# Gathered rows spread to the end of an expert loop, and late fetches begun in its last part and paced by product columns

## The chip, the cores and the metric

One core of one Trainium2 chip runs the whole program. The metric is the device time of one execution in microseconds (us). Engines are named as in the profile: PE (TensorE; PEld its weight loads), DVE (VectorE), ACT (ScalarE), POOL (GpSimd), SP (SyncE, which here issues most DMAs).

## The reference

Two transformer blocks follow one another on 512 tokens, in four tiles of 128, with a width of 1024. What the change touches is the expert layer of the first block and what comes behind it:

```python
def peer_experts(xc, idx, gates, u, v):
    u_sel = jnp.take(u, idx, axis=0)
    act = jax.nn.gelu(jnp.einsum("chkd,cd->chk", u_sel, xc))
    v_sel = jnp.take(v, idx, axis=0)
    return jnp.einsum("chk,chkd->cd", act * gates, v_sel)
...
    x = x + FFN_RESIDUAL_WEIGHT * swiglu(rms_norm_2(x, ffn1_norm[l]), ffn1_w_gate[l], ffn1_w_up[l], ffn1_w_down[l])
    h = rms_norm_2(x, mix_norm[l])
    proj = h @ w_in[l]
    (q_lat, kv_lat, k_rope, fq, fk, fv, f_logit, g_mla, g_fox) = jnp.split(proj, split_points, axis=-1)
```

Each token chooses 128 of the experts (8 heads, 16 each). An expert is a row of u and a row of v, 1024 wide.

## The kernel before

**The expert layer** treats the four tiles in three ways. For three of them the activations of all experts are computed as products with u, 128 experts at a time (`u_tile`, `u_steps`), 128 such groups. Slots 0 and 1 then multiply them by the gates (`hf`, split into `hh` and `hl`) and by v, also group by group: these are the V products in PSUM (`acc`). The gathered tile (GT = 3) uses neither: for each of its 128 choices one indirect DMA on POOL's queue fetches for 128 tokens the row of peer_u (`gather_u`), DVE makes the dot product, and later a second one fetches the row of peer_v (`gather_v`), which DVE adds into `c.ht[GT]`. A fetch is 128 x 1024 floats, 512 KB, into a buffer of tag row, of which there are four. The late tile (LT = 2) takes part in the u products, but its activations are spilled to memory (`act_d`), and class `Late` fetches them back by token, one column of 128 x 1 an indirect DMA (`fetch`, into `c.lact`), and the row of peer_v that belongs to it (`vrow`), which DVE adds into h_late (`add`). `Late.steps(n)` does n of these fetches, acts up to 16 (`AHEAD`) before rows.

**The loop.** u products run 36 (LAG) groups ahead of V products; the loop over i has both until group 91 and V products alone in its last 36 iterations. Behind each iteration `spent(n)` asks for as many of the 256 gathers as n is of `GSPAN`. A weight tile (512 KB) is split into a high half on ACT (wh, L98) and a low half on DVE (wl, L103); `hh` and `hl` have three buffers. Every eighth iteration loads the gates `gt`, 1 MB.

**Behind the loop** `features` transposes the three tiles into feature-major rows, and ffn1 follows for these three: 44 products of 24 matmuls (`mm`, 384 columns) for gate and up, alternately, and eight columns (`dn`) of 66. `Late.steps` is called in both, and then in attention's beginning, until the late tile is complete; from there on it runs by itself as a fourth tile (`last`, L1129 by the wt tiles, full fp32).

**In attention** the products of the late tile are `todo[0]` (the latent part lat of 360 columns, tile tl in the profile: query and key latents, k_rope, forget logits) and `todo[1]` to `todo[3]` (fq, fk, fv), each made by `last` in one of two PSUM banks of tag mm. Then come four z gates, and after them in the code the norms of lat, its transposes (L1218 to L1225), rope, the log-sigmoid of the forget logits (lf, L1240 to L1254) and its running sum cp (L1257).

**Order.** Instructions are put in order at build time by a scheduler that simulates a timeline, engine by engine; `keep_in_program_order` pins the indirect DMAs among each other, which share POOL's queue. Semaphores do the rest at run time, and each engine works in order.

## Time and profile before

| what | value |
| --- | --- |
| median of 3 runs | 2740.44 us (2737.12 to 2742.59) |
| profiled execution | 2743.67 us, its span 2741.5 us |
| mean granted PE clock | 0.964 |
| PE, DVE, ACT, POOL busy | 2546.8, 1815.2, 914.9, 822.2 us |

The span runs from the first instruction to the last one of the profiled execution. Busy time is summed over an engine's instructions; an engine can be busy 93% of the span and still set the end in some stages only, so the stages are read one by one. By the trace the u and V loop with both kinds of products runs until 1335, V products alone until 1433, ffn1 until 1786, and attention's last products of the late tile until about 2145.

### The profile page before, as it was taken

What the parts mean: (1) busy time and instruction counts of PE and PEld (TensorE: products, weight loads), DVE (VectorE), ACT (ScalarE), POOL (GpSimd) and SP (SyncE); (2) the same over time, 40 slices, a digit from 0 to 9 for tenths busy, and PEclk for the clock granted to TensorE, in tenths of its full rate; (3) what the DMA queues carried; (4) which work ended last, traced back from release to release, by engine and by line L of the source; (5) the groups of instructions that cost most, each with busy time, mean ns of one, the idle gap of its engine ahead of it and who ended that gap; (6) DMA issues with size and microseconds to landing.
All of it is one profiled execution on the core that took longest, in us unless ns stands there. A gap on an engine that the chain in (4) does not pass through costs nothing.

```text
span 2741.5 us, 34004 instructions
## 1 busy us (share of the span) xinstructions
PE 2546.8 (93%) x12098; PEld 2088.0 (76%) x12098; DVE 1815.2 (66%) x3710; ACT 914.9 (33%) x1531; POOL 822.2 (30%) x686
## 2 busy tenths in 40 slices
PE   8979988998999989999998988888998999999999
PEld 7955455787888888889878888887444877788887
DVE  7986996997878877874676777776113675443322
ACT  4232011453333333344453322233013554422321
POOL 0000244333444444420006888672000340211100
PEclk9989999999999999999999999998999899999999
DMA  4213138889999989985664778786885313222232
GB/s 173 93 62 102 62 104 280 297 288 324 348 326 339 345 317 331 342 301 176 202 205 132 270 267 269 263 275 230 297 286 176 102 36 108 93 93 100 90 104 75
DMA packets 196921, 567.77 MB, mean 207 GB/s; under 512 B 23240, under 2 KB 60488, under 8 KB 194576
## 3 DMA queue, kind: packets, MB, share of 16 engines
q1 hardware_dynamic: 132464, 355.60, 38.1%
q0 software_dynamic: 59392, 201.42, 21.2%
q10 hardware_dynamic: 4896, 8.57, 0.8%
q8 instruction: 96, 1.57, 0.2%
q14 instruction: 73, 0.60, 0.1%
HBM read 534.05 MB, written 31.47 MB: 206 GB/s over the span
## 4 chain that ended last, share of the span: by engine, by line
PE 63%; DMA 13%; DVE 11%; POOL 6%; issue 5%; ACT 2%; SPq 0%; POOLq 0%; DVEq 0%; ACTq 0%
PE u L419 13%; DMA wf<-u_t 5%; DMA vrow<-peer_v,lidx 5%; PE v L79 4%; PE v L80 4%; PE v L81 3%; PE mm L79 3%; PE mm L80 3%; PE mm L81 3%; POOL lact L715 3%; PE x L960 3%; DMA row<-peer_u,gidx 2%; POOL vrow L735 2%; PE pj L79 2%; PE pj L81 2%
## 5 line engine op out<-in xcount | busy, mean ns | idle before, releaser
L103 DVE TENSOR_TENSOR wl<-wf,wh 128x1024 fp32r<-128x1024 f32 (+2 forms) x438 | 532.5, 1216 | 251.7 <-ACT wh L98 244.9
L98 ACT CAST wh<-wf 128x1024 fp32r<-128x1024 f32 (+2 forms) x438 | 452.9, 1037 | 593.3 <-PE mm L80 163.2
L419 PE MATMUL u<-xh,wh 128*128 128x384 f32 x760 | 267.1, 351 | 38.7 <-ACT wh L98 38.7
L81 PE MATMUL mm<-hh,wl 128*128 128x384 f32 (+1 forms) x704 | 262.0, 372 | 22.6 <-DVE wl L103 22.6
L419 PE MATMUL u<-xh,wl 128*128 128x384 f32 x760 | 265.5, 349 | 8.5 <-DVE wl L103 8.5
L79 PE MATMUL mm<-hh,wh 128*128 128x384 f32 (+1 forms) x704 | 261.0, 372 | 4.3 <-DVE rows L683 2.3
L419 PE MATMUL u<-xl,wh 128*128 128x384 f32 x760 | 264.1, 347 | 0.0
L80 PE MATMUL mm<-hl,wh 128*128 128x384 f32 (+1 forms) x704 | 262.6, 373 | 0.0
L564 POOL DMA_INDIRECT row<-peer_u,gidx x128 | 171.3, 1338 | 251.5 <-DVE jkd L567 226.7
L575 POOL DMA_INDIRECT row<-peer_v,gidx x128 | 173.5, 1355 | 206.8 <-DVE h_tok L578 188.3
L80 PE MATMUL v<-wl,hh 128*128 128x512 f32 x512 | 204.1, 399 | 0.0
L81 PE MATMUL v<-wh,hl 128*128 128x512 f32 x512 | 200.7, 393 | 0.0
L724 DVE SCALAR_TENSOR_TENSOR h_late<-vrow,lact,h_late 128x1024 f32<-128x1024 f32 x128 | 164.4, 1284 | 54.2 <-DMA vrow<-peer_v,lidx 53.4
L419 PEld LDWEIGHTS u<-xh,wh 128*128 128x128 f32 x760 | 149.4, 197 | 46.7 <-ACT wh L98 42.8
L567 DVE SCALAR_TENSOR_TENSOR jkd<-row,xg 128x1024 bf16<-128x1024 f32 x128 | 156.5, 1222 | 37.9 <-DMA row<-peer_u,gidx 37.3
L419 PE MATMUL u<-xf,w 128*128 128x384 f32 x496 | 172.8, 499 | 6.8 <-ACT spill L427 6.8
L735 POOL DMA_INDIRECT vrow<-peer_v,lidx x128 | 155.9, 1218 | 46.4 <-issue 29.3
L81 PEld LDWEIGHTS mm<-hh,wl 128*128 128x128 f32 x704 | 135.9, 193 | 40.1 <-DVE wl L103 25.1
L578 DVE SCALAR_TENSOR_TENSOR h_tok<-row,gwt,h_tok 128x1024 f32<-128x1024 f32 x128 | 163.9, 1280 | 3.5 <-DMA row<-peer_v,gidx 2.7
L715 POOL DMA_INDIRECT lact<-act_d,laid x128 | 153.9, 1203 | 38.8 <-issue 35.3
L419 PEld LDWEIGHTS u<-xh,wl 128*128 128x128 f32 x760 | 148.9, 196 | 14.7 <-DVE wl L103 14.5
L525 POOL TENSOR_TENSOR dk<-CE,posf 128x800 f32<-128x800 f32 x32 | 48.7, 1553 | 352.1 <-DVE posf L521 352.1
(437 smaller groups left out, 5302.2 us busy)
## 6 DMA issues: line engine op xcount, KB each, us to landing
wf<-peer_v SPq DMA_DIRECT2D x128, 512.0 KB, 5.0
wf<-u_t SPq DMA_DIRECT2D x95, 512.0 KB, 6.0
wf<-f_g SPq DMA_DIRECT2D x44, 512.0 KB, 3.3
wf<-f_u SPq DMA_DIRECT2D x44, 512.0 KB, 3.6
w<-u_t SPq DMA_DIRECT2D x33, 512.0 KB, 4.0
gates_d<-stg SPq DMA_DIRECT2D x16, 1024.0 KB, 6.9
gt<-gates_d SPq DMA_DIRECT2D x16, 1024.0 KB, 12.7
wf<-f_d SPq DMA_DIRECT2D x32, 512.0 KB, 3.6
```

What stands on the lines that cost most here:

```text
L79: nc.tensor.matmul(ps, lh, rh, start=start, stop=False)
L80: nc.tensor.matmul(ps, lh, rl, start=False, stop=False)
L81: nc.tensor.matmul(ps, ll, rh, start=False, stop=stop)
L98: nc.scalar.copy(out=h, in_=f)
L103: (nc.vector if lo == "v" else nc.gpsimd).tensor_tensor(out=l, in0=f, in1=h.bitcast(F32), op=ALU.subtract)
L419: mm = nc.tensor.matmul(ps3, l, r, start=k == 0 and m == 0, stop=k == KD - 1 and m == len(mms) - 1)
L564: dm = nc.gpsimd.indirect_dma_start(out=row, out_offset=None, in_=A["peer_u"], in_offset=bass.IndirectOffsetOnAxis(ap=gidx[:, s:s + 1], ax ...
L575: dm = nc.gpsimd.indirect_dma_start(out=row, out_offset=None, in_=A["peer_v"], in_offset=bass.IndirectOffsetOnAxis(ap=gidx[:, s:s + 1], ax ...
L578: nc.vector.scalar_tensor_tensor(out=hh, in0=row, scalar=gwt[:, s:s + 1], in1=hh, op0=ALU.mult, op1=ALU.add)
L715: dm = c.nc.gpsimd.indirect_dma_start(out=c.lact[:, s:s + 1], out_offset=None, in_=acts, in_offset=bass.IndirectOffsetOnAxis(ap=c.laid[:, ...
L724: c.nc.vector.scalar_tensor_tensor(out=self.h, in0=self.pending.pop(0), scalar=c.lact[:, s:s + 1], in1=self.h, op0=ALU.mult, op1=ALU.add)
L735: dm = c.nc.gpsimd.indirect_dma_start(out=row, out_offset=None, in_=self.A["peer_v"], in_offset=bass.IndirectOffsetOnAxis(ap=c.lidx[:, s:s ...
```

## The change

What it does, part by part:

1. The users of a gathered row (`dot`, `add`) are written two rows behind its DMA (list `rows`, `take`), and the gates are multiplied onto the activations at the first v row of a head.
2. `GSPAN` and `spent` spread the gathers to the loop's end: 4, 7 and 3 parts of 752 for an early, a middle and a late iteration, where it was 2, 3 and 1 of 310.
3. In the last 35 iterations `c.late.fetch()` fetches one column of the late tile's activations each.
4. `Late.beside(columns)` takes the place of `Late.steps(n)`: one fetch for each 3520 columns of products. For a gate or up product (24 x 384 columns) that is 2.6 where it was 3, for a `dn` column (66 x 384) 7.2 where it was 9.
5. `lact` is eight tiles of 16 columns, where it was one of 128 (allocated elsewhere, not shown).
6. `features(GT)` comes behind the features of slots 0 and 1.
7. In attention the norm of lat, rope on k and the log-sigmoid move in between `last(*todo[0])` and `last(*todo[1])`; the transposes, cp, the decay's store and its transposes in between `todo[1]` and `todo[2]`.

```diff
-        def gather_u(s):
+        def fetch(src, s):
             row = c.xp.tile([P, D], F32, tag="row", name="row", bufs=4)
-            dm = nc.gpsimd.indirect_dma_start(out=row, out_offset=None, in_=A["peer_u"], in_offset=bass.IndirectOffsetOnAxis(ap=gidx[:, s:s + 1], axis=0))
+            dm = nc.gpsimd.indirect_dma_start(out=row, out_offset=None, in_=src, in_offset=bass.IndirectOffsetOnAxis(ap=gidx[:, s:s + 1], axis=0))
             tc.keep_in_program_order(dm)
+            return row
+
+        def dot(row, s):
             jk = pe.tile([P, D], BF16, tag="jk", name="jkd", bufs=1)
             nc.vector.scalar_tensor_tensor(out=jk, in0=row, scalar=1.0, in1=xg, op0=ALU.mult, op1=ALU.mult, accum_out=gact[:, s:s + 1])
             if s % TOPK == TOPK - 1:
                 hs = slice(s - TOPK + 1, s + 1)
                 nc.scalar.activation(out=gact[:, hs], in_=gact[:, hs], func=AF.Gelu_apprx_tanh)
+
+        def add(row, s):
+            if s % TOPK == 0:
+                hs = slice(s, s + TOPK)
                 nc.vector.tensor_tensor(out=gwt[:, hs], in0=gact[:, hs], in1=G8[:, GT, s // TOPK, :], op=ALU.mult)
-
-        def gather_v(s):
-            row = c.xp.tile([P, D], F32, tag="row", name="row", bufs=4)
-            dm = nc.gpsimd.indirect_dma_start(out=row, out_offset=None, in_=A["peer_v"], in_offset=bass.IndirectOffsetOnAxis(ap=gidx[:, s:s + 1], axis=0))
-            tc.keep_in_program_order(dm)
             hh = c.ht[GT]
             nc.vector.scalar_tensor_tensor(out=hh, in0=row, scalar=gwt[:, s:s + 1], in1=hh, op0=ALU.mult, op1=ALU.add)
+
+
+        rows = []
 
         gathered = 0
 
         def gathers(upto):
             nonlocal gathered
             while gathered < min(upto, 2 * NE):
-                (gather_u if gathered < NE else gather_v)(gathered % NE)
+                n = gathered % NE
+                rows.append((dot, fetch(A["peer_u"], n), n) if gathered < NE else (add, fetch(A["peer_v"], n), n))
                 gathered += 1
+                if len(rows) > 2 or gathered == 2 * NE:
+                    take()
+            while gathered == 2 * NE and rows:
+                take()
+
+        def take():
+            what, row, n = rows.pop(0)
+            what(row, n)
...
-            GSPAN = 2 * EARLY + 3 * (NE - LAG) + LAG - 8
+            GSPAN = 4 * EARLY + 7 * (NE - LAG) + 3 * (LAG - 4)
 
             def spent(n):
                 gathers(G0 + (2 * NE - G0) * n // GSPAN)
 
             for i in range(EARLY):
                 u_tile(LAG - EARLY + i)
-                spent(2 * (i + 1))
+                spent(4 * (i + 1))
...
                 if i < NE - TAIL:
                     v_products(range(2))
                     tail.clear()
-                spent(2 * EARLY + i + 1 + 2 * min(i + 1, NE - LAG))
+                spent(4 * EARLY + 3 * (i + 1) + 4 * min(i + 1, NE - LAG))
+                if i > NE - LAG:
+                    c.late.fetch()
...
-                    if slot in (GT, 0):
+                    if slot == 0:
                         tp = up.tile([P, 4, P], F32, tag="u", name="tr", bufs=2)
                     else:
-                        tp = pv.tile([P, 4, P], F32, tag=f"v{slot - 1}{k4}", name="tr", bufs=1)
+                        tp = pv.tile([P, 4, P], F32, tag=f"v{int(slot == GT)}{k4}", name="tr", bufs=1)
...
-            features(GT)
             for t in range(2):
                 v_products([t])
                 for n in range(2):
                     hs = c.ht[t][:, n * 512:(n + 1) * 512]
                     nc.vector.tensor_tensor(out=hs, in0=hs, in1=acc[t][n], op=ALU.add)
                 features(t)
+            features(GT)
...
+STEP = 3520
...
-        self.acts = self.rows = self.added = 0
+        self.acts = self.rows = self.added = self.time = 0
         self.pending = []
 
     def fetch(self):
         c, s = self.c, self.acts
+        if s == NE:
+            return
         acts = c.act_d.rearrange("e i t -> (e i t)").unsqueeze(1)
-        dm = c.nc.gpsimd.indirect_dma_start(out=c.lact[:, s:s + 1], out_offset=None, in_=acts, in_offset=bass.IndirectOffsetOnAxis(ap=c.laid[:, s:s + 1], axis=0))
+        dm = c.nc.gpsimd.indirect_dma_start(out=c.lact[s // AHEAD][:, s % AHEAD:s % AHEAD + 1], out_offset=None, in_=acts, in_offset=bass.IndirectOffsetOnAxis(ap=c.laid[:, s:s + 1], axis=0))
         c.tc.keep_in_program_order(dm)
         self.acts += 1
 
@@ -720,8 +739,9 @@
         c, s = self.c, self.added
         if s % AHEAD == 0:
             hs = slice(s, s + AHEAD)
-            c.nc.vector.tensor_tensor(out=c.lact[:, hs], in0=c.lact[:, hs], in1=c.lg[:, hs], op=ALU.mult)
-        c.nc.vector.scalar_tensor_tensor(out=self.h, in0=self.pending.pop(0), scalar=c.lact[:, s:s + 1], in1=self.h, op0=ALU.mult, op1=ALU.add)
+            a = c.lact[s // AHEAD]
+            c.nc.vector.tensor_tensor(out=a, in0=a, in1=c.lg[:, hs], op=ALU.mult)
+        c.nc.vector.scalar_tensor_tensor(out=self.h, in0=self.pending.pop(0), scalar=c.lact[s // AHEAD][:, s % AHEAD:s % AHEAD + 1], in1=self.h, op0=ALU.mult, op1=ALU.add)
         self.added += 1
...
+    def beside(self, columns):
+
+        self.time += columns
+        self.steps(int(self.time // STEP))
+        self.time %= STEP
...
         def steps(m):
             if late:
-                c.late.steps(m)
+                c.late.beside(m * 3 * n)
...
-            steps(3)
+            steps(KD)
...
-                steps(3)
+                steps(m)
...
-                c.late.steps(4)
+                c.late.beside(KD * 3 * N1)
...
-                    c.late.steps(4)
+                    c.late.beside(3 * 4 * 3 * n)
...
-            for w, n, evac in todo:
-                last(w, n, evac)
+            last(*todo[0])
...
+            for tt in range(4):
+                for i, (o, n) in enumerate(parts):
+                    sq = tp.tile([P, T], F32, tag="t", name="lsq", bufs=3)
+                    nc.scalar.activation(out=sq[:, 0:n], in_=lat[:, tt, o:o + n], func=AF.Square, accum_out=ls[:, i, tt:tt + 1])
...
+            l12 = ls.rearrange("p a t -> p (a t)")
+            rsqrt(c, l12, l12, (QR, KVR, ROPE))
+            for i, (o, n) in enumerate(parts):
+                nc.vector.tensor_tensor(out=lat[:, :, o:o + n], in0=lat[:, :, o:o + n], in1=ls[:, i].unsqueeze(2).to_broadcast([P, 4, n]), op=ALU.mult)
...
+            rotate(nc.vector, krr, kr, cos, sin, tmp4, 4)
...
+            nc.vector.tensor_tensor(out=lf, in0=lat[:, :, LAT - MH:LAT], in1=bf.unsqueeze(1).to_broadcast([P, 4, MH]), op=ALU.add)
+            nc.scalar.activation(out=e, in_=lf, func=AF.Abs)
+            nc.scalar.activation(out=e, in_=e, func=AF.Exp, scale=-1.0)
...
+            nc.vector.scalar_tensor_tensor(out=lf, in0=y, scalar=-2.0, in1=lf, op0=ALU.mult, op1=ALU.add)
+            last(*todo[1])
+            for tt in range(4):
+                ts = slice(tt * P, (tt + 1) * P)
+                t4 = trp()
+                nc.tensor.transpose(t4[:, 0, :], lat[:, tt, 0:P], c.ident)
+                nc.tensor.transpose(t4[:QR - P, 1, :], lat[:, tt, P:QR], c.ident)
...
+            cp = big("cp")
+            for j in range(4):
+                nc.tensor.matmul(cp[:MH, j * P:], lf[:, j, :], tri[:, 0:T - j * P], start=(j == 0), stop=(j == 3), skip_group_check=True)
+            nc.scalar.mul(out=c8, in_=cp[:MH, :], mul=8.0)
+            nc.sync.dma_start(out=cd, in_=c8)
+            t4 = trp()
+            for tt in range(4):
+                nc.tensor.transpose(t4[:, tt, 0:MH], c8[:, tt * P:(tt + 1) * P], c.ident[:MH, :MH])
+            nc.scalar.copy(out=cq, in_=t4[:, :, 0:MH])
+
+            last(*todo[2])
+            last(*todo[3])
```

**POOL's order, whole.** The first rows are those of before, the second ones those of after; row is a gathered row of tile GT, lact and vrow are the late tile's fetches, sqs the sums of squares at the head of ffn1.

```order
L564 DMA row<-peer_u,gidx 128x1024 x128
L575 DMA row<-peer_v,gidx 128x1024 x128
L781 TENSOR_TENSOR sqs<-sqs,sq 128x384 x7
L715 DMA lact<-act_d,laid 128x1 x16
L735 DMA vrow<-peer_v,lidx 128x1024
L715 DMA lact<-act_d,laid 128x1
```

```order
L564 DMA row<-peer_u,gidx 128x1024 x128
L564 DMA row<-peer_v,gidx 128x1024 x101
L734 DMA lact_75<-act_d,laid 128x1
L564 DMA row<-peer_v,gidx 128x1024
L734 DMA lact_75<-act_d,laid 128x1 x2
L564 DMA row<-peer_v,gidx 128x1024
...
L734 DMA lact_77<-act_d,laid 128x1 x3
L807 TENSOR_TENSOR sqs<-sqs,sq 128x384 x7
L755 DMA vrow<-peer_v,lidx 128x1024 x20
L734 DMA lact_77<-act_d,laid 128x1
L755 DMA vrow<-peer_v,lidx 128x1024
```

229 gathers stand as before; the other 27 alternate with 35 act fetches behind the first of these (one row stands between most of them), and all of them stand ahead of the sums of squares. Then 20 row fetches follow at once where 16 act fetches stood. On DVE the users of these 27 gathers stand between the gates (hf) of iterations 99 and 121, one at a time; before, all users stood ahead of those of iteration 80. Ahead of the end of ffn1's sixth `dn` column DVE now has 96 row adds (and POOL, up to the rows that these need, 76 act fetches behind the sums of squares), and none between there and ffn1's end; before, 89 stood ahead of that column and 5 behind it.

**DVE's order at the head of ffn1**, from the norm's steps to the first hidden tile (sg), before and then after.

```order
L142 TENSOR_TENSOR rt_11877<-na_11878,nt_11879 128x3
L805 TENSOR_TENSOR rt_11877<-rt_11877,r_fin_11701 128x3
L791 TENSOR_SCALAR dg_11890<-ident_65,rt_11877 128x128
L791 TENSOR_SCALAR dg_11893<-ident_65,rt_11877 128x128
L791 TENSOR_SCALAR dg_11896<-ident_65,rt_11877 128x128
L860 TENSOR_TENSOR sg_11933<-mm_11908,rs_11888 128x384
L860 TENSOR_TENSOR sg_12009<-mm_11984,rs_11888 128x384
```

```order
L103 TENSOR_TENSOR wl_12199<-wf_12196,wh_12198 128x1024
L744 SCALAR_TENSOR_TENSOR h_late_88<-vrow_11979,lact0_75,h_late_88 128x1024
L136 TENSOR_SCALAR na_11920<-ss_11915 128x3
L103 TENSOR_TENSOR wl_12243<-wf_12240,wh_12242 128x1024
L744 SCALAR_TENSOR_TENSOR h_late_88<-vrow_11981,lact0_75,h_late_88 128x1024
L138 RECIPROCAL nt_11921<-nt_11921 128x3
L139 TENSOR_TENSOR na_11920<-na_11920,nt_11921 128x3
L140 TENSOR_TENSOR na_11920<-na_11920,nt_11921 128x3
L141 TENSOR_SCALAR na_11920<-na_11920 128x3
L744 SCALAR_TENSOR_TENSOR h_late_88<-vrow_12018,lact0_75,h_late_88 128x1024
L142 TENSOR_TENSOR rt_11919<-na_11920,nt_11921 128x3
```

Before, the first row add (h_late) stood behind the first three hidden tiles; now the first stands ahead of the norm's first step on ss, and six stand ahead of the first sg.

**PE's order in attention**, from the sum ss of the late tile's norm on, before and then after. tm with 512 columns are here fk's and fv's products (the tiles of fq and lat stand just before), tr transposes.

```order
L1177 MATMUL ss_16121<-ones_63,sqs_13799 128x1
L1129 MATMUL tm_16189<-w32_16190,xn_15650 128x512 x2
L1129 MATMUL tm_16189<-w32_16194,xn_15650 128x512 x2
L1129 MATMUL tm_16189<-w32_16198,xn_15650 128x512 x2
L1129 MATMUL tm_16189<-w32_16202,xn_15650 128x512 x2
L1149 MATMUL tr_16183<-ident_65,fsq_16168 128x128 x4
L1129 MATMUL tm_16228<-w32_16229,xn_15650 128x512 x2
```

```order
L1175 MATMUL tr_16274<-ident_65,fsq_16259 128x128 x4
L1256 MATMUL tr_16280<-ident_65,tl_14620 128x128
L1257 MATMUL tr_16280<-ident_65,tl_14620 64x128
L1258 MATMUL tr_16280<-ident_65,tl_14620 128x128
L1256 MATMUL tr_16290<-ident_65,tl_14620 128x128
L1257 MATMUL tr_16290<-ident_65,tl_14620 64x128
L1258 MATMUL tr_16290<-ident_65,tl_14620 128x128
L1266 MATMUL cp_16320<-tl_14620,lf_16210 8x512
L1266 MATMUL cp_16320<-tl_14620,lf_16210 8x384
L1266 MATMUL cp_16320<-tl_14620,lf_16210 8x256
L1266 MATMUL cp_16320<-tl_14620,lf_16210 8x128
L1155 MATMUL tm_16333<-w32_16334,xn_15657 128x512 x2
```

Before, fk's products (tm_16189) stood right behind ss, and tl's transposes and cp came behind the z products; now two tiles' transposes of tl and cp stand between fq's transposes and fk's products (tm_16333).

## Rows read from the trace of the kernel before

**Rows 1.** The page: busy time of each engine, and the chain that ended last.

```profile
PE 2546.8 (93%) x12098; PEld 2088.0 (76%) x12098; DVE 1815.2 (66%) x3710; ACT 914.9 (33%) x1531; POOL 822.2 (30%) x686
PE 63%; DMA 13%; DVE 11%; POOL 6%; issue 5%; ACT 2%; SPq 0%; POOLq 0%; DVEq 0%; ACTq 0%
```

**Rows 2.** Stretches: their length, then busy us (instructions) by engine, PE clock, DMA share, GB/s.

```profile
615.00:1126.00 511.00, 468.91 (x2288) 425.90 (x2287) 404.34 (x509) 186.59 (x326) 221.40 (x171) 0.95 0.94 335
1126.00:1213.00 87.00, 81.95 (x412) 74.50 (x411) 69.87 (x74) 32.40 (x58) 37.80 (x27) 0.98 0.92 325
1213.00:1335.00 122.00, 122.00 (x626) 112.09 (x625) 60.45 (x74) 52.40 (x91) 0.00 (x0) 1.00 0.59 192
1335.00:1433.00 98.00, 98.00 (x426) 78.80 (x425) 69.78 (x101) 47.49 (x70) 0.00 (x0) 1.00 0.65 208
1433.00:1786.00 353.00, 302.80 (x1622) 295.66 (x1620) 262.10 (x321) 109.60 (x156) 260.62 (x211) 0.94 0.71 238
2053.00:2145.00 92.00, 74.91 (x234) 42.53 (x232) 37.79 (x143) 29.92 (x77) 10.13 (x21) 0.83 0.47 154
```

**Rows 3.** Waits in ffn1, 1433 to 1786: us in all, times, longest.

```profile
DVE h_late L724 <- DMA vrow<-peer_v,lidx: 46.7, 32, 3.8
DVE lact L723 <- DMA lact<-act_d,laid: 27.3, 5, 8.1
PE mm L81 <- DVE wl L103: 22.6, 8, 7.0
PE dn L81 <- DVE wl L103: 20.4, 7, 7.4
```

**Rows 4.** Timeline of POOL: gather 229 and gather 256 (start us, us, instruction, idle before).

```profile
1123.72 0.94 POOL L575 DMA_INDIRECT row<-peer_v,gidx  x1 [2.71 <-DVE h_tok L578]
1203.94 0.94 POOL L575 DMA_INDIRECT row<-peer_v,gidx  x1 [0.65 <-DVE h_tok L578]
```

**Rows 5.** Timeline of ACT: its last spill to act_d.

```profile
1330.72 0.33 ACTq L429 DMA_DIRECT2D act_d<-spill  x1
```

**Rows 6.** Groups on DVE, 1335 to 1405: busy us, mean ns, idle before.

```profile
L103 DVE TENSOR_TENSOR wl<-wf,wh 128x1024 fp32r<-128x1024 f32 x25 | 30.6, 1225 | 5.5 <-ACT wh L98 4.1
L654 DVE TENSOR_TENSOR hf<-act,gt 128x256 f32<-128x256 f32 x25 | 10.6, 425 | 0.9
```

**Rows 7.** The page's costliest groups: the user of a gathered peer_v row.

```profile
L578 DVE SCALAR_TENSOR_TENSOR h_tok<-row,gwt,h_tok 128x1024 f32<-128x1024 f32 x128 | 163.9, 1280 | 3.5 <-DMA row<-peer_v,gidx 2.7
```

**Rows 8.** A stretch of the u and V loop with high DMA traffic, columns as in rows 2.

```profile
800.00:850.00 50.00, 47.21 (x241) 42.70 (x239) 40.47 (x59) 17.57 (x34) 21.26 (x18) 1.00 0.98 353
```

**Rows 9.** Timeline of POOL in ffn1: sums of squares, first and last row fetch.

```profile
1450.44 11.05 POOL L781 TENSOR_TENSOR sqs<-sqs,sq 128x384 f32<-128x384 f32 x7 [245.56 <-ACT sq L780]
...
1482.21 0.94 POOL L735 DMA_INDIRECT vrow<-peer_v,lidx  x1 [0.30 <-issue]
...
1761.88 1.81 POOL L735 DMA_INDIRECT vrow<-peer_v,lidx  x1 [0.30 <-issue]
```

**Rows 10.** Groups on POOL, 1461 to 1763.

```profile
L715 POOL DMA_INDIRECT lact<-act_d,laid x106 | 127.4, 1202 | 32.1 <-issue 28.9 <-DMA vrow<-peer_v,lidx 3.0
L735 POOL DMA_INDIRECT vrow<-peer_v,lidx x91 | 114.9, 1262 | 27.8 <-issue 20.1 <-DMA vrow<-peer_v,lidx 4.9 <-DVE sg L860 0.9
```

**Rows 11.** Waits of PE, 2045 to 2145.

```profile
PE tr L1218 <- DVE tl L1214: 11.0, 1, 11.0
PE tr L1262 <- DVE kvl L1225: 2.9, 1, 2.9
```

**Rows 12.** Timeline of PE: a qp product before and one after the wait for kvl.

```profile
2118.04 0.38 PE L80 MATMUL qp<-wl,qnh 128*128 128x480 f32 x1
...
2129.25 0.60 PE L80 MATMUL qp<-wl,qnh 64*128 64x480 f32 x1
```

**Rows 13.** Timeline of DVE: first and last step of the log-sigmoid chain.

```profile
2055.24 0.19 DVE L1240 TENSOR_TENSOR lf<-tl,rowc 128x32 f32<-128x32 f32 x1 [0.69 <-ACT tl L1134]
...
2063.82 0.19 DVE L1254 SCALAR_TENSOR_TENSOR lf<-lfy,lf 128x32 f32<-128x32 f32 x1
```

More of the change, by code (lines that the diff above doesn't have):

```diff
@@ L867, in ffn @@
             split(c, t, gh[:, j, :], gl[:, j, :])
-            steps(3)
+            steps(KD)
         if then:
@@ L1450, in emit @@
         c.laid = per.tile([P, NH * TOPK], U32, name="laid")
-        c.lact = per.tile([P, NH * TOPK], F32, name="lact")
+        c.lact = [per.tile([P, AHEAD], F32, name=f"lact{g}") for g in range(NE // AHEAD)]
         c.lg = per.tile([P, NH * TOPK], F32, name="lg")
```

49 lines of the change are left out of this document (21 added, 28 removed).

## The prediction

> **What bounds the kernel now.** I read the page's busy shares and its chain first: TensorE (PE) is busy 93% of the span, and the chain that ended last lies on PE for 63%, on DMA for 13%, on VectorE (DVE) for 11% and on GpSimd (POOL) for 6% [rows 1]. Most of the time is products that the change leaves alone; only stages in which PE sits idle can give anything. The table of stretches finds them [rows 2]: 615 to 1126 (u and V products with the gathers; PE idle 42 us), 1433 to 1786 (ffn1; idle 50) and 2053 to 2145 (last products of attention; idle 17). From 1213 to 1433 PE has no idle time at all, and DMA is at 0.59 and 0.65. The reader is to see this imbalance: gathers crowd the DMA engines up to 1213 (0.94, 0.92), nothing is gathered in the next 220 us, and then ffn1 carries all late fetches.
>
> The waits tell what ends PE's idle time in ffn1 [rows 3]: wl, the low half of a split weight, made on DVE, 43 us together. Behind it DVE stands for a landing row (46.7 us) or for an act fetch (27.3 us in five long waits). DVE works in order, so a wl queued behind such a wait comes late.
>
> **The change part by part.** *Loop with u products.* The order up to gather 229 of 256 is the same in both kernels: the scheduler runs gathers ahead of their place. That gather is issued at 1123.72, the last one at 1203.94 [rows 4]. Gathers 230 to 256 now stand behind the first act fetch on POOL, and that fetch reads what the last u tile spills, which goes out at 1330.72 [rows 5]. So 27 gathers (13.8 MB) leave 1126 to 1213. There PE idles 5 us of 87 at a clock of 0.98; behind it, where no gathers run, it idles none at 1.00 [rows 2]: 5 + 0.02 x 87 = 7. I take **−7** (bounds −9 to −4). That the users stand two rows behind their fetch changes no order up to there, so I cost it at nothing; what it could touch is PE's idle time in 615 to 1126, and DMA at 0.94 speaks against it.
>
> *V-only loop.* The 27 gathers and 35 act fetches now run in the iterations without u products, which fill PE, 98 of 98 us [rows 2]: some 35 in 98 us, 2.8 each. DVE's users stand between iterations 99 and 121, 1.23 rows to an iteration. Three prices. (a) DVE: wl 1.23, hf 0.42, hl (same size and type) 0.42 [rows 6], and 1.23 users of 1.28 [rows 7]: 3.65 us listed, some 3.5 with the overlap of neighbours, so 22 x 0.7 = 15, less some us by which the hh buffers run ahead: +8 to +15. (b) DMA: an iteration moves 512 KB of V weights, 1.23 rows of 512 KB and 128 KB of gates, 1.27 MB; at the most that I find in the trace, 353 GB/s [rows 8], 3.6 us: 22 x 0.8 = +17. (c) POOL: the last row is its 57th DMA after about 1330; at 1.25 us each (the pace of acts in ffn1, below) it lands about 1408, at 1.53 (that of rows and acts mixed) about 1425, where its user's place in the old pace is about 1397: +6 to +23, when PE's lead of some 5 us is used up. The three lie beside each other. I take **+18**, between (b) and the upper (c), bounds +4 to +28. V ends near 1444 then, 1433 before.
>
> The Trainium skill, Perfetto Trace Analysis, Roofline, says that a core alone on its memory domain can pull more than its share of 358 GB/s, bounded by its DMA engines at about 435. This trace's fullest stretch shows 353 at 0.98 of the engines' time, so nothing here comes near the page's bound. By its 435 an iteration's 1.27 MB would take 2.9 us (an estimate), (b) would fall away, the term would be about +12 and the sum 6 lower.
>
> *Between the loops.* features(GT) comes last, so the gathered tile's transposes and its splits follow the dense ones: a few evacuations of under half a us, **+2** (1 to 4).
>
> *ffn1.* POOL paces it: its seven sums of squares end at 1461.5, its first row fetch goes out at 1482.21, after 16 acts, the last one of ffn1 at 1761.88 [rows 9]. Between 1461 and 1763 it issued 106 acts and 91 rows, idle before them mostly by its own issue [rows 10]: 197 in 301 us, 1.53 each. As a model: V end + 28 (sums) + 204 steps x 1.53 + 6 (landing) = V end + 346; measured 353. Now 35 acts are there already, so 20 row fetches go out at once, and columns of products pace fewer of both: in the order 96 row adds stand ahead of ffn1's sixth last-stage column, with 76 acts, 172 DMAs: V end + 28 + 2 + 172 x 1.53 + 6 = V end + 299. The last two columns, without late work, are 66 products each; by PE's 302.8 us for 1622 instructions [rows 2] that is 12 us each: V end + 323. PE's own work bounds it at 303. The eight tiles of lact end the 27.3 us of act waits [rows 3], in which a multiply of 16 columns waited for a later fetch into the same tile. Against it: six row adds stand ahead of ffn1's first hidden tile on DVE, the first one ahead of the norm's own steps, so that tile can't start before V end + 36. From 353 to 323 is −30; for these early adds I give back 3: **−27**, bounds −45 (all waits gone, near PE's floor) and −15.
>
> *Attention's beginning.* 32 rows are left there now, 34 before, at the same place: **0** (−5 to +3).
>
> *The latent part moved.* In 2045 to 2145 PE waits 11.0 us for tl's norm and 2.9 for kvl [rows 11], and after the first the qp products show 0.60 us where one shows 0.38 before the second wait [rows 12]. A mean clock of 0.83 over 92 us [rows 2] is 0.17 x 92 x 2 = 31 us at the lower level; some 13 of these are waits, the other 18 cost half of themselves, 9. Waits and clock, −23, may go, as qnh and kvl are made under fk, fv and z. But in the new order fk's products stand behind tr(tl) and cp, and these wait for the norm of tl and for the log-sigmoid chain, which took DVE from 2055.24 to 2064 when it ran under the fq and fk products [rows 13], 11 us after the products' end; with the norm's steps between them I put the new stall at 13 to 17, and the clock may fall there as it did at 2103. Gain 23, loss 15 and half speed behind it: **0**, bounds −10 to +14.
>
> *Sum.* −7 + 18 + 2 − 27 + 0 + 0 = −14. The profiled execution took 2743.67, its span is 2741.5: 2727.5 of span, 2729.7 of time. The runs' median is 3.2 below the profiled execution, so I say **2727**.
>
> **Rivals.** *A, the forecast*: the V loop slower, ffn1 shorter by more. 2727, chance 0.45.
> *B, the V loop nearly free*: DMA has room there (0.65 [rows 2]), POOL issues at 1.25, only DVE's +8 is left, and ffn1 goes nearer to its floor, −35: −7 + 8 + 2 − 35 = −32, **2709**. Against it: rows and acts mixed took 1.53. 0.2.
> *C, ffn1 doesn't gain*, the one on the other side: DVE still stands in order behind rows that land some 5 us after their issue, in the same six buffers. If landing and buffers set the pace and not POOL's count, the five act waits only move to other rows: −7 + 18 + 2 + 0 = +13, **2754**. It decides where POOL is seen idle in ffn1 while DVE waits for rows. For it: 32 waits for rows, up to 3.8 us. Against: POOL idles mostly for its issue [rows 3, 10]. 0.2.
> *D, it does little*: the scheduler re-orders what the code spreads (229 gathers unmoved, about five adds to a column as before), and a gain in ffn1 of only 13 meets the V loop's cost: **2740**, 0.15.
>
> **How the numbers follow.** 0.2%, 5.5 us, is about what a measurement of this kernel can tell from no change. The predicted time is A's, and A's own range, from the bounds of the V loop and of ffn1 that partly cancel, is 2712 to 2742. The range for 8 in 10 reaches into B and to C's time: 2703 to 2755. Faster: A 0.37 of its 0.45 (below 2735), B 0.2, D 0.03, together 0.6. Same: A 0.06, D 0.09, C 0.03, together 0.18. Slower: C 0.17, D 0.03, A 0.02, together 0.22.
>
> **What would show it.** Gather 230 goes out after the last spill; PE has no idle time in the loop behind gather 229; the V loop's period goes from 2.8 to about 3.5, V ending near 1444 (B: 1434); POOL's first row fetch of ffn1 is at about V end + 30; DVE never waits on lact in ffn1; ffn1 is 323 us long, PE's waits for wl half of 43. In attention PE waits some 15 us for cp or its bank near the middle, and not 11 before qp, which then run at 0.38. The prediction is wrong if the V loop costs over 28 us (users too late for the loop's end, and the tail waits for the gathered tile), if the six early adds hold ffn1's first hidden tile so long that PE stands over 20 us there, or if attention's new stall outlasts its chain.

## The result and the profile after

The changed kernel takes 2755.72 us (median of 12 runs, 2742.47 to 2764.05) where the kernel before took 2735.39 in the same comparison (12 runs): a ratio of 1.0073, 95% interval 1.0055 to 1.0092. It is slower by some 20 us; 2727 had been forecast, with a range of 2703 to 2755. The profiled execution took 2757.47 us, its span is 2755.7 and the mean granted clock 0.959. The stretches of [rows 2], of the changed kernel and at the same cuts:

```profile
615.00:1126.00 511.00, 469.49 (x2287) 426.52 (x2286) 405.17 (x510) 186.50 (x326) 216.89 (x171) 0.95 0.94 335
1126.00:1213.00 87.00, 87.00 (x449) 80.25 (x449) 44.81 (x54) 35.43 (x62) 0.28 (x1) 1.00 0.60 187
1213.00:1335.00 122.00, 122.00 (x621) 111.29 (x620) 60.22 (x74) 50.36 (x89) 2.82 (x3) 1.00 0.60 187
1335.00:1433.00 98.00, 79.80 (x296) 59.12 (x295) 78.55 (x102) 34.82 (x52) 74.61 (x60) 0.91 0.88 291
1433.00:1786.00 353.00, 313.31 (x1692) 303.73 (x1691) 276.05 (x339) 120.61 (x171) 225.87 (x179) 0.95 0.76 253
2053.00:2145.00 92.00, 71.70 (x212) 37.29 (x211) 33.52 (x130) 26.40 (x57) 6.75 (x14) 0.82 0.47 150
```

From 1126 to 1213 PE now idles 0 of 87 us at a clock of 1.00, where it idled 5 at 0.98. From 1335 to 1433 it does 79.8 us of work where it did 98.0, at 0.91 and not 1.00, while POOL went from nothing to 74.6 us.

Stretches with fixed cuts mix stages once the ends move. So each trace, of these kernels and of all those below, is cut at the starts and ends of the same named instructions: the last u product, the last V product, the first sg of ffn1, the eighth `rows<-dn` of ffn1, the first x product of the late tile, the first qp and the first dn of ffn2. "head" is from the V products' end to ffn1's first hidden tile, "late end" from ffn1's end to the late tile's first x product (its last row adds and its copy), "heads" what follows from the first qp to the first `rows<-dn` of ffn2. The other stages agree with before within 2.5 us and are left out.

| us, one profile each | u loop | V loop | head | ffn1 body | late end | heads | ratio to before, 95% interval |
| --- | --- | --- | --- | --- | --- | --- | --- |
| before | 1021.6 | 104.5 | 34.3 | 317.5 | 137.3 | 513.6 | |
| after | 1014.9 | 132.9 | 46.4 | 289.4 | 132.7 | 525.3 | 1.0073 (1.0055 to 1.0092) |
| after_again | 1012.1 | 129.1 | 45.7 | 284.7 | 132.8 | 522.4 | 1.0047 (1.0031 to 1.0064) |
| gathers_first | 1019.6 | 121.4 | 46.4 | 305.6 | 139.0 | 522.5 | 1.0005 (0.9985 to 1.0025) |
| one_fetch | 1019.3 | 124.1 | 37.0 | 320.9 | 157.7 | 526.5 | 1.0063 (1.0041 to 1.0085) |
| no_latmove | 1017.1 | 132.5 | 46.4 | 296.3 | 138.7 | 515.6 | 0.9990 (0.9971 to 1.0010) |
| first_nolat | 1023.5 | 128.3 | 46.4 | 299.8 | 141.8 | 522.3 | 1.0010 (0.9991 to 1.0030) |
| late_head | 1008.6 | 130.1 | 37.1 | 280.4 | 136.0 | 521.7 | 0.9985 (0.9968 to 1.0001) |
| paced_acts | 1030.9 | 104.3 | 47.2 | 286.0 | 133.0 | 522.2 | 0.9990 (0.9972 to 1.0007) |
| paced_head_nolat | 1027.1 | 103.6 | 36.7 | 285.3 | 135.2 | 519.8 | 0.9907 (0.9877 to 0.9938) |
| paced_head | 1024.7 | 103.6 | 36.6 | 300.4 | 140.6 | 522.3 | 0.9922 (0.9896 to 0.9949) |
| latmove_only | 1021.6 | 104.5 | 33.5 | 330.2 | 144.1 | 519.2 | 1.0056 (1.0029 to 1.0083) |
| paced_spread | 1010.6 | 135.9 | 47.4 | 294.3 | 142.5 | 524.4 | 1.0043 (1.0020 to 1.0065) |
| spread_only | 1021.8 | 103.6 | 36.7 | 319.8 | 150.6 | 521.6 | 1.0045 (1.0030 to 1.0060) |
| half_dve | 1012.8 | 136.6 | 47.4 | 297.0 | 141.6 | 525.6 | 1.0020 (0.9999 to 1.0041) |
| half_both | 1017.9 | 133.2 | 46.7 | 298.0 | 139.3 | 523.0 | 0.9997 (0.9978 to 1.0017) |
| repairs_moved | 1020.6 | 103.6 | 36.6 | 296.4 | 142.6 | 518.0 | 0.9915 (0.9892 to 0.9938) |
| repairs_unmoved | 1021.9 | 103.6 | 36.7 | 298.0 | 142.3 | 522.1 | 0.9898 (0.9874 to 0.9922) |

The kernel before had medians of 2735 to 2771 us in the different comparisons, so ratios compare kernels across rows. Rows measured on one chip in one comparison are gathers_first to first_nolat; after_again, late_head, paced_acts and paced_head_nolat; paced_head to spread_only; and the last four. The ffn1 body, the late end and the u loop compare less well across rows than the V loop and the head do: paced_head_nolat and repairs_unmoved are one file, with bodies of 285.3 and 298.0.

Against before, the V loop is 28 us longer and the head 12, ffn1's body 28 shorter, the late end 5 shorter, the heads 12 longer. The V loop, seen on POOL (timeline: start us, us, instruction, idle before):

```profile
1125.35 0.94 POOL L564 DMA_INDIRECT row<-peer_v,gidx  x1 [2.61 <-DVE h_tok L580]
1331.57 1.44 POOL L734 DMA_INDIRECT lact<-act_d,laid  x1 [205.29 <-DMA wf<-peer_v]
1333.32 1.13 POOL L564 DMA_INDIRECT row<-peer_v,gidx  x1 [0.30 <-DVE hl L103]
...
1419.32 1.17 POOL L564 DMA_INDIRECT row<-peer_v,gidx  x1 [0.30 <-issue]
...
1426.92 0.95 POOL L734 DMA_INDIRECT lact<-act_d,laid  x1 [0.30 <-issue]
```

POOL stands 205 us for the first act fetch, which needs what the last u tile spilled, and then issues 62 fetches without a break, 1.56 us from one to the next; the last row is the 57th. The users and the weights come late behind them (waits, 1327 to 1457):

```profile
DVE h_tok L580 <- DMA row<-peer_v,gidx: 17.1, 8, 7.1
PE v L80 <- DVE wl L103: 15.3, 9, 4.2
```

Over the V loop DVE is busy 101.7 us where it was 73.9, and it stands 17.1 us for rows. From 1343 to 1359, where no row keeps it waiting, it is full (third figure behind the length), PE is not, and an iteration takes 3.0 us, 2.8 before:

```profile
1343.00:1359.00 16.00, 14.13 (x55) 11.33 (x55) 15.69 (x22) 5.95 (x9) 13.56 (x9) 0.89 0.87 288
```

The head, on DVE (timeline), with the first late row add ahead of the norm's first step:

```profile
1492.18 1.28 DVE L744 SCALAR_TENSOR_TENSOR h_late<-vrow,lact,h_late 128x1024 f32<-128x1024 f32 x1 [5.66 <-DMA vrow<-peer_v,lidx]
1493.38 0.15 DVE L136 TENSOR_SCALAR na<-ss 128x3 f32<-128x3 f32 x1
...
1503.35 1.02 DVE L886 TENSOR_TENSOR sg<-mm,rs 128x384 f32<-128x384 f32 x2
```

DVE stands 5.66 us for a landing row, then adds it, and only then may the norm begin that all of ffn1's evacuations need; the five other early adds stand between the norm's steps and ahead of sg. The waits in ffn1 that answer to [rows 3] (1433 to 1786), and the groups on POOL that answer to [rows 10] (1526 to 1763):

```profile
DVE h_late L744 <- DMA vrow<-peer_v,lidx: 27.7, 17, 5.7
DVE lact L743 <- DMA lact<-act_d,laid: 24.0, 4, 9.1
```

```profile
L734 POOL DMA_INDIRECT lact<-act_d,laid x76 | 96.8, 1274 | 23.2 <-issue 22.0 <-DMA vrow<-peer_v,lidx 1.2
L755 POOL DMA_INDIRECT vrow<-peer_v,lidx x75 | 94.5, 1260 | 23.8 <-issue 15.5 <-DVE h_late L744 2.8 <-DVE wl L103 2.4
```

The act waits are still there, 24.0 us for 27.3. POOL still paces: 151 fetches in 237 us, 1.57 each. The 20 rows ahead of them took 1.9 us each (1487.5 to 1525.1), as POOL comes to wait for buffers that DVE's adds free. And PE's waits in attention (1780 to 2180), in place of [rows 11]:

```profile
PE tr L1175 <- DVE krr L1066: 11.8, 1, 11.8
...
PE qp L79 <- DVE qt L1325: 7.4, 1, 7.4
PE cp L1266 <- DVE lf L1251: 1.0, 1, 1.0
```

The wait of 11.0 for tl's norm has become one of 11.8 at fq's transposes, which stand on DVE behind the norm, rope and log-sigmoid of the latent part; a wait of 7.4 for the query heads follows, where kvl's was 2.9. As in [rows 12], a qp product takes 0.38 us ahead of that wait and 0.60 behind it, and in the heads' stage, some 70 us behind the first qp, the granted clock is 0.89 where it was 1.00 (70 us of before, then of after):

```profile
2120.49 0.38 PE L80 MATMUL qp<-wl,qnh 128*128 128x480 f32 x1
...
2133.21 0.60 PE L80 MATMUL qp<-wl,qnh 128*128 128x480 f32 x1
```

```profile
2186.20:2256.20 70.00, 67.91 (x471) 55.74 (x472) 55.81 (x271) 39.18 (x124) 24.48 (x44) 1.00 0.11 35
2188.80:2258.80 70.00, 66.87 (x409) 54.27 (x410) 49.95 (x241) 35.79 (x112) 16.20 (x30) 0.89 0.11 36
```

### The profile page after: what moved, and what is told of

Read it like the earlier page. It is cut to its first block, busy times and chain, and to the rows that moved or that the text cites. A ratio compares the mean times of both kernels' runs of the same rounds, so it can differ in the third digit from the quotient of the medians.

```text
span 2755.7 us, 33980 instructions
## 1 busy us (share of the span) xinstructions
PE 2556.0 (93%) x12098; PEld 2091.1 (76%) x12098; DVE 1812.1 (66%) x3710; ACT 915.6 (33%) x1531; POOL 823.9 (30%) x686
## 3 DMA queue, kind: packets, MB, share of 16 engines
q8 instruction: 96, 1.57, 0.2%
## 5 line engine op out<-in xcount | busy, mean ns | idle before, releaser
L564 POOL DMA_INDIRECT row<-peer_u,gidx x128 | 180.3, 1408 | 242.4 <-DVE jkd L570 218.2
L564 POOL DMA_INDIRECT row<-peer_v,gidx x128 | 165.1, 1290 | 179.1 <-DVE h_tok L580 151.5
L79 PE MATMUL v<-wh,hh 128*128 128x512 f32 x512 | 157.0, 400 | 2.5 <-ACT wh L98 2.5
```

Source lines behind the costliest of these rows:

```text
L79: nc.tensor.matmul(ps, lh, rh, start=start, stop=False)
L564: dm = nc.gpsimd.indirect_dma_start(out=row, out_offset=None, in_=src, in_offset=bass.IndirectOffsetOnAxis(ap=gidx[:, s:s + 1], axis=0))
```

## The experiments

**The theory**: three parts cost, each by itself: the 35 act fetches with the 27 rows in the V loop, the early row adds in ffn1's head, and the move of the latent part. **The rivals**: in the V loop, DVE's users of the rows, or the rows' bytes alone; for the time at the end, the spreading itself and not the latent part. Line numbers of after are used; the parts left out of a diff are as in the change.

### Which part of the V loop's traffic costs

**gathers_first** asks for all gathers before the first act fetch, so that the scheduler puts all 256 beside the u products as before.

```diff
+                if i == NE - LAG:
+                    gathers(2 * NE)
                 if i > NE - LAG:
                     c.late.fetch()
```

> The changed kernel, but all 256 gathers are asked for before the first act fetch, so that they run beside the u products again and the V-only loop has 35 act fetches alone. Main theory (the 27 gathers cost the V-only loop its 28 us, by DVE's in-order waits for rows and by DMA): end of the u products to end of the V products falls from 132.9 to 104 to 107 us, the u loop gets its 5 us back, the time is about 23 us under the changed kernel's, near 2733. Rival (the act fetches on POOL and their small packets slow the weights): the V-only loop stays over 120 us and the time stays above 2745.

**one_fetch** leaves the rows in the V loop and one act fetch of the 35 (the others follow in ffn1).

```diff
-                if i > NE - LAG:
+                if i == NE - LAG + 1:
                     c.late.fetch()
```

> The changed kernel with one act fetch in the V-only loop instead of 35: the 27 gathers still stand behind it on POOL, but nothing between them. If it is POOL's queue (62 fetches at 1.5 us) that made the rows late, the V-only loop falls from 132.9 by 10 or more, to about 118. If rows, DVE and DMA alone cost it, it stays at 125 to 135. In both cases ffn1 must do 34 more act fetches: first hidden tile to its last column goes from 289 back to about 315.

With the acts alone the V loop is 17 us longer than before (121.4; in first_nolat below, whose loop is the same, 24: 128.3), with the rows alone 20 (124.1), with both 28 (132.9). The theory of gathers_first, 104 to 107, failed. The rows alone nearly fill the DMA engines and DVE (70.3 of 80 us), with POOL half free (stretches, 1340 to 1420, columns as in rows 2; after, then one_fetch):

```profile
1340.00:1420.00 80.00, 61.80 (x225) 44.66 (x224) 66.04 (x86) 25.03 (x37) 64.48 (x51) 0.91 0.91 306
```

```profile
1340.00:1420.00 80.00, 67.15 (x257) 50.17 (x256) 70.27 (x89) 28.47 (x43) 38.26 (x25) 0.94 0.95 334
```

The acts alone (gathers_first) leave DMA half idle, and PE still waits. ACT stands ahead of each cast of hh:

```profile
1340.00:1420.00 80.00, 69.19 (x268) 51.06 (x267) 44.72 (x69) 30.44 (x44) 33.43 (x30) 0.96 0.56 173
```

```profile
1346.56 0.41 ACT L98 CAST hh<-hf 128x256 fp32r<-128x256 f32 x1 [4.39 <-issue]
1352.28 0.41 ACT L98 CAST hh<-hf 128x256 fp32r<-128x256 f32 x1 [4.36 <-issue]
1357.35 0.40 ACT L98 CAST hh<-hf 128x256 fp32r<-128x256 f32 x1 [3.71 <-issue]
```

An iteration (one such cast each) takes 5 to 6.5 us, 2.8 before, while POOL issues act fetches one after the other, 35 from 1333.60 to 1381.33, 1.40 apart. A weight tile is cast 12 to 15 us after its issue, but it isn't the load that is late. The tiles issued at 1349.21 and 1354.92 pass in some 2.3 us each and are through within 3.3 us of their issue, as before; between them DMA moves nothing:

```profile
1350.10:1352.40 2.30, 1.88 (x9) 1.17 (x7) 0.00 (x0) 0.12 (x1) 1.79 (x2) 1.00 0.75 228
1352.40:1355.80 3.40, 2.05 (x8) 1.40 (x9) 2.08 (x3) 1.23 (x2) 2.70 (x3) 1.00 0.02 0
1355.80:1358.20 2.40, 1.27 (x6) 0.70 (x4) 0.42 (x1) 0.85 (x2) 1.88 (x2) 1.00 0.72 219
```

What ACT waits for, no view tells ("issue"). The hh cast at 1346.56 needs hf, made by 1342.15, and the buffer that PE's product left at 1343.35: it begins 3.2 us late. Such stalls of over half a us add up to 29 us in this loop and to 30 in first_nolat, where one takes 19.1. The V loops of before, of the change (both profiles), of late_head and of no_latmove have none. So it is not shown that the acts by themselves cost the changed kernel anything, and what causes these stalls stays open.

### Is it DVE's user, the bytes, or POOL's pace

**half_dve** adds only half of each of the last 27 rows (it leaves out the other half of these additions); **half_both** also fetches only 2 KB for each of these rows (and from another place of the table).

```diff
-            hh = c.ht[GT]
-            nc.vector.scalar_tensor_tensor(out=hh, in0=row, scalar=gwt[:, s:s + 1], in1=hh, op0=ALU.mult, op1=ALU.add)
+            m = D if s < 101 else D // 2
+            hh = c.ht[GT][:, 0:m]
+            nc.vector.scalar_tensor_tensor(out=hh, in0=row[:, 0:m], scalar=gwt[:, s:s + 1], in1=hh, op0=ALU.mult, op1=ALU.add)
```

> The changed kernel, in which DVE adds only the left half (512 columns) of each of the 27 rows gathered in the V-only loop; the rows are still fetched whole. It leaves out half of these additions. If DVE's time for the users is what the V-only loop lacks (27 x 0.6 us), its length falls from 129 to 133 to about 115. If it is the transfers and their landing, it stays at 127 to 133.

> As the run before it, and each of these 27 fetches brings 512 columns too (half a row, from another place of the table), so that both DVE's work and the bytes are halved: 6.9 MB less in the V-only loop. It uses other values than the reference for these columns. If bytes and landing are what the loop lacks, it falls to 112 to 118 here and not in the run before; if POOL's count of fetches is, it stays near 127 in both; if DVE, both fall alike.

The V loop stays at 136.6 and 133.2, but neither settles the question. Both profiles have the stalls of gathers_first, 15 us of them in each, which the change has not; in half_dve PE stands 10.7 us behind a single one (ACT's timeline, then a wait of PE):

```profile
1415.68 0.40 ACT L98 CAST hh<-hf 128x256 fp32r<-128x256 f32 x1 [10.60 <-remote]
...
PE v L79 <- ACT wh L98: 16.0, 5, 10.7
```

These two executions, 2776.95 and 2774.10, are also 7 and 10 us above their kernels' medians. In half_both DMA is no longer full, and POOL is, with its gaps of 0.3 us behind each of 55 fetches:

```profile
1340.00:1420.00 80.00, 65.23 (x251) 48.71 (x250) 55.86 (x87) 26.74 (x38) 63.41 (x55) 0.95 0.78 243
```

The total ratios of these two, 1.002 and 0.9997, lie below those of the change (1.0073 and 1.0047), as they would if half the users and half the bytes did save time in the V loop. So none of the three, DVE's users, the bytes, POOL's pace, is shown to be innocent or to be enough. What the change's own trace shows is DVE: full where rows are there, and standing where they are late.

### Is it the number of act fetches or that they follow without a break

**paced_acts** is gathers_first with each act fetch held back until its iteration's `hf` is there, by a copy on POOL that writes the fetch's column first.

```diff
-    def fetch(self):
+    def fetch(self, behind=None):
...
+        if behind is not None:
+            c.nc.gpsimd.tensor_copy(out=c.lact[s // AHEAD][:, s % AHEAD:s % AHEAD + 1], in_=behind[:, 0:1])
...
                 if i > NE - LAG:
-                    c.late.fetch()
+                    c.late.fetch(hf)
```

> All 256 gathers before the act fetches, as in the run that had them alone in the V-only loop (121 us), but each act fetch goes out behind a one-column copy on POOL that reads that iteration's gates product hf, so that they come one to an iteration and not back to back. Theory (35 fetches back to back slow the loop's weight loads, whose waits came at 5 to 6 us an iteration while the fetches ran, and 2.8 behind them): the V-only loop falls to 104 to 108 us, ffn1 stays as it was in that run. Rival (each fetch costs the same whenever it comes, about 0.5 us): it stays at 118 to 122.

**paced_spread** paces the acts in this way and leaves the rows in the V loop.

> The changed kernel with its 27 late gathers, but act fetches one to an iteration as in the paced run. It shows what the gathers alone cost in the V-only loop when the act fetches cost nothing: by the run with one act fetch, 124 us from the u products' end to the V products' end, so 120 to 126, where the changed kernel has 129 to 133 and the paced run without gathers 104. Time 0.998 to 1.001 of the changed kernel's, that is 1.003 to 1.005 of the kernel before. If it is the act fetches that make the rows late, it falls to 112 or less.

In paced_acts the V loop is back at 104.3: all 35 fetches are there, 2.58 us apart, and PE is full at a clock of 1.00.

```profile
1340.00:1420.00 80.00, 79.84 (x342) 63.75 (x341) 55.86 (x85) 39.81 (x59) 51.68 (x57) 1.00 0.69 223
```

So 35 fetches cost the loop nothing when they keep its pace; the four profiles of the kernels with all repairs, which have them too, show 103.6. Not all of it reaches the time: against after_again, on the same chip, the V loop is 25 us shorter, the u loop, which has the 27 rows back, 19 longer, and the medians are 13 apart. In paced_spread the loop stays at 135.9, where 120 to 126 was expected: with rows and paced acts in turn on its queue POOL is busy 62.5 of 80 us, and DVE stands 22.0 us for rows, 17.1 in the change. Pacing helps once the rows are gone; the rows cost 20 us by themselves (one_fetch).

### The head and the latent part

**late_head** pins the late tile's first multiply behind what is written ahead of it, so that no row add stands ahead of ffn1's first sg.

```diff
-            c.nc.vector.tensor_tensor(out=a, in0=a, in1=c.lg[:, hs], op=ALU.mult)
+            put = c.nc.vector.tensor_tensor(out=a, in0=a, in1=c.lg[:, hs], op=ALU.mult)
+            if s == 0:
+                c.tc.keep_in_program_order(put)
```

> The changed kernel, with the first multiply of late factors pinned behind the first hidden tile on DVE, so that no row add stands ahead of ffn1's norm (none ahead of the first sg, six in the changed kernel). Theory (the adds in DVE's order cost the head of ffn1 12 us, since the first one waits for a row that lands 15 us behind the sums of squares' start): V end to the first hidden tile falls from 46 to 35 to 38 us, and 8 to 12 us of it are left in the time, 0.997 of the changed kernel. Rival: POOL's count sets ffn1's end, so the ffn1 body grows by the same 10, no gain in the time.

**after_again** is the changed kernel once more, on the chip of late_head.

> The changed kernel itself again, to stand on the same chip as the three runs that follow. Expected 1.005 to 1.009 of the kernel before, as in the result; stages as there: V products end 130 to 134 us after the u products, 46 from there to ffn1's first hidden tile, 290 to 300 to ffn1's last column.

Head 45.7 to 37.1, ratio 1.0047 to 0.9985: 0.6%, some 17 us, for one pinned instruction that holds back all six early adds. Of these, 9 are in the head and 4 in ffn1's body (284.7 to 280.4); where the others are is not shown. The norm's first step comes 32.5 us behind the V loop's end, 36.4 in the change, and from it to sg there are 4.6 us, 10.0 in the change (DVE, timeline):

```profile
1480.61 0.16 DVE L136 TENSOR_SCALAR na<-ss 128x3 f32<-128x3 f32 x1 [1.79 <-PE ss L829]
...
1485.25 1.02 DVE L888 TENSOR_TENSOR sg<-mm,rs 128x384 f32<-128x384 f32 x2 [1.09 <-ACT rs L835]
...
1490.45 1.28 DVE L746 SCALAR_TENSOR_TENSOR h_late<-vrow,lact,h_late 128x1024 f32<-128x1024 f32 x1
```

**no_latmove** is the change with attention's latent part as before (part 7 undone); **first_nolat** is gathers_first with that; **latmove_only** is the kernel before with part 7 alone.

```diff
-            last(*todo[0])
...
+            for w, n, evac in todo:
+                last(w, n, evac)
```

> The changed kernel with the latent part of attention as before (its norm, rope, log-sigmoid, transposes and running sum behind the z gates again). Theory: the move gained nothing up to the first query product (75.2 us from the late tile's end in both) and lost 12 us behind it, where PE's clock was 0.87 from 2185 to 2250: so the time is about 12 us under the changed kernel's, near 2744. Rival: the 12 us behind it are a matter of the one profiled execution, and the time is within 4 us of the changed kernel's.

> Both undone: all gathers before the act fetches, and the latent part as before. What stays of the change: act fetches in the V-only loop, eight tiles of lact, pacing by columns, order of features. If the gains add up: 23 + 12 under the changed kernel's, about 2721, and 14 under the kernel before. If the ffn1 body's gain of 28 is taken back by the later stages (late rows are done at 1887 in both kernels), it is near the kernel before, 2735.

> The kernel before with the latent part moved and nothing else. Theory: 75 us from the late tile's end to the first query product as before, a wait of PE of 7 to 8 us behind it for the query heads, 5 to 9 us slower, 1.002 to 1.003. Rival: 0.999 to 1.001.

The answers don't agree on a size. The change without the move is no slower than before (0.9990, against 1.0073 and 1.0047 with it), and the move alone is slower (1.0056); but gathers_first and first_nolat, on one chip, don't differ (1.0005 and 1.0010). No pair shows a gain by the move that is clear of the intervals; what it loses lies between 0 and 0.8%.

**spread_only** is the change without the act fetches in the loop; the scheduler then puts all 256 gathers beside the u products.

> The changed kernel without any act fetch in the V-only loop, so that its scheduler puts all gathers beside the u products: what is left is pacing by columns, eight tiles of lact, the order of features and the moved latent part. V-only loop 104, head 36 (no row add ahead of the first hidden tile). If the 35 early act fetches are what shortened ffn1, its body is near 317 again and the late tail ends later (50 row adds are left behind ffn1, 34 before), 1.003 or more. If the eight tiles and the pacing shortened it, it stays at 290 to 300 and the time is 0.997 to 1.000.

The V loop costs nothing there (103.6), and the ratio, 1.0045, is that of the latent move alone (1.0056, on the same chip). Against that kernel, whose ffn1 is that of before, ffn1's body is 10 us shorter (319.8 and 330.2) and the late end 6 longer (150.6 and 144.1): `beside` does fewer fetches in a column than `steps` did (78 adds are done by ffn1's end, 94 before), and the fetches that the V loop took over are missing. With them, in paced_spread on the same chip, the body is 294.3, 25 us less; one_fetch and no_latmove, on one chip, show 25 too (320.9 and 296.3).

### All repairs together

**paced_head** is paced_acts with the pin of late_head; **paced_head_nolat** is that with the latent part as before. **repairs_moved** and **repairs_unmoved** are the same two files once more, on one chip.

> Gathers first, paced act fetches, first late multiply behind the first hidden tile, but with the latent part moved as in the changed kernel. It differs from the run with the three repairs (0.9907 of the kernel before) by the move alone. Theory (the move gives nothing up to the first query product and 5 to 9 us are lost behind it): 0.993 to 0.995. Rival (the move is neutral, what is seen behind it varies with the clock): 0.990 to 0.992.

> The three repairs together: gathers first, act fetches one to an iteration, no row add ahead of ffn1's first hidden tile, and the latent part as before. If each theory holds (V-only loop 106, head 36, ffn1 300, the rest as before) it is some 15 us under the kernel before, 0.993 to 0.997 of it. If ffn1's and the late rows' rate on POOL set the end of attention's beginning (last add near 1890 in every kernel), it is within 0.998 to 1.002.

> Gathers first, paced act fetches, first late multiply behind the first hidden tile, latent part moved as in the changed kernel; now on one chip with the next run, which differs by the move alone. Theory: the move costs 5 to 9 us behind the first query product, so 1.002 to 1.003 of the next run, and 0.991 to 0.994 of the kernel before. Rival: no difference between the two.

> The same with the latent part as before: 0.989 to 0.992 of the kernel before, and 0.997 to 0.998 of the run above; by the rival, equal to it.

All four are below both kernels, by 0.8 to 1.0% against before: 28 us in repairs_unmoved (2736.14, before 2764.47). V loop and head are at 103.6 and 36.6 or 36.7 in each, and the V loop's stretch has what the change was to bring, acts in it and PE full:

```profile
1340.00:1420.00 80.00, 80.00 (x344) 64.45 (x343) 55.81 (x84) 39.85 (x58) 59.14 (x63) 1.00 0.69 212
```

With and without the latent move, 0.9915 and 0.9898 on one chip, their intervals overlap.

## Why the prediction was wrong

By its own steps, with the changed kernel's profile against that of before:

- *Loop with u products, −7*: right. Gather 230 goes out behind the last spill, PE idles 0 us behind gather 229, and the loop ends 5 us earlier.
- *V-only loop, +18*: the mechanism was there, the size was 28.4, just beyond the upper bound of 28. The last row went out as price (c) had it: it is the 57th fetch, issued at 1419.32, which with landing is the 1425 that 1.53 us each gave, and its +23 was in the text. The step that failed is "The three lie beside each other. I take +18, between (b) and the upper (c)". On DVE, which takes its work in order, the prices add up in part: its own users fill it at 3.0 us an iteration, and it stands 17.1 us for late rows besides. Not priced at all was PE's granted clock, 0.91 in this stretch, in which it waited. Price (b) counts a KB as 1000 bytes, where an iteration moves 1.30 MB, and takes 353 GB/s for the most in the trace, where 870.7 to 920.7 shows 371; the two make it +15, no other choice.
- The reading by the Trainium skill, Perfetto Trace Analysis, Roofline (435 GB/s for a core alone), by which (b) would fall away: with the rows alone, DMA moved 334 GB/s at 0.95 of its engines' time and the loop was 20 us longer. The page's figure was not reached over those 80 us. Whether DMA or DVE, itself nearly full there, held that loop up is not separated.
- *Between the loops, +2*: right; the head without an early add (37.1 in late_head) is 2.8 longer than before. But the 323 of the next term holds this +2 already, so the sum counts it twice.
- *ffn1, −27*: the body gave −28.1, but V's end to ffn1's end only −16, where −25 was forecast with the +2. Two steps failed. "For these early adds I give back 3": they cost 13, 9 of them in the head and 4 in the body, by late_head against after_again, and 17 in the time. POOL's 172 fetches then went at 1.61 us each up to the last row at 1763.4, not at 1.53. "The eight tiles of lact end the 27.3 us of act waits": 24.0 are left, in four waits for five. The reading behind it was wrong: in the kernel before each of the five multiplies began 0.1 to 0.2 us after its own sixteenth column had landed (the one at 1584.8 after 1584.68), so no later fetch into the tile held it. What shortened the body was POOL's count, the 35 acts fetched early: 25 us on each of two chips. Two readings were off without harm: the −30 sets a modelled 323 against a measured 353, where the model gave 346, and ffn1's last row fetch went out at 1770.9, behind the 1761.88 of [rows 9].
- *Attention's beginning, 0*: −4.6, inside its bounds.
- *The latent part, 0*: until the first qp product it was 0 (75.2 us in both); the new stall, put at 13 to 17, was 11.8 and 1.0. "Waits and clock, −23, may go" failed: PE waits 7.4 us for the query heads, and the qp products behind that wait take 0.60 us again. Behind the first qp the heads' stage was 12 us longer in this profile, inside the term's bounds and the largest miss of the sum. Over all profiles it is 522.7 on the mean of the 13 with the move (518.0 to 526.5) and 518.7 of the 5 without (513.6 to 522.3), so the move explains a part of it at most. The wait for qt is one part; the rest, the clock of 0.89 in it, is open.

The sum by stages is −5 + 28 + 3 − 19 − 5 + 12 = +14, what the profiled executions show (2757.47 and 2743.67). The medians are 20 apart. Against the forecast's −14 the misses are +2 in the loop with u products, +10 in the V loop, +9 in head and ffn1, −5 in attention's beginning and +12 in the latent part. Of the rivals none came true: ffn1 did gain (not C), the V loop was not free (not B), and the V loop cost more than ffn1 gave (not D). That C's 2754 lies next to the 2755.72 measured is luck. Slower came by the forecast's own mechanism with its V term past the bound, by the early adds, and by the heads' stage, of which the cause is open. The early adds had been named as what would make the prediction wrong, though PE stood 17 us in the head (6 before), less than the 20 named there.

## What to carry to other kernels

Work that is moved into a stage without idle time on its bounding engine is best spaced by that stage's own progress: a queue that is only kept in order empties itself at its full speed as soon as its first wait ends, and here the paced fetches cost the stage nothing. Before adding in-order work to an engine, look for the one norm or scale that a whole stage waits for, and keep everything that waits for a DMA behind it; here one pinned instruction was worth some 17 us. And where several prices fall on one in-order engine, its own work and its waits for late data, add them up instead of choosing a value between them.

## What was unexpected in the hardware

With 35 act fetches of 128 x 1 floats, 0.02 MB in all, issued without a break, an iteration of the V loop took 5 to 6.5 us while the DMA engines were listed half idle. In gathers_first and in paced_acts the same 25 us show it:

```profile
1345.00:1370.00 25.00, 18.32 (x66) 12.65 (x65) 8.63 (x14) 6.18 (x10) 19.60 (x18) 0.93 0.47 144
```

```profile
1345.00:1370.00 25.00, 25.00 (x109) 20.13 (x108) 17.90 (x28) 12.36 (x18) 19.57 (x22) 1.00 0.67 201
```

144 GB/s with fetches 1.40 us apart, 201 at 2.58 us apart. It looks as if the small fetches slowed the 512 KB loads, but the tiles passed at 219 to 228 GB/s and were through 3.3 us after their issue; they were only asked for late. What stood was ACT, for up to 19.1 us at a time, with its inputs there. The changed kernel's own trace, with 62 fetches without a break, has no such stall; why the four profiles with it have it, no run here shows.
